# The turned residual on its way through the scratch: written whole, read back in 128-byte runs

## The chip, the core and the metric

The kernel runs on one core of one Trainium2 chip. The metric is the device time of one execution in microseconds (us). Before the change the median of three runs is 1144.76 us (1144.58 to 1144.79). The core has five engines with a queue of instructions each: TensorE (PE, matmuls), VectorE (DVE), ScalarE (ACT), GpSimd (POOL) and SyncE (SP). SyncE does nothing here but issue DMA transfers; ScalarE issues some too, between its own instructions. An engine works through its queue in order, so an instruction that waits holds up all that is queued behind it.

## The reference

A decoder of two layers over 512 tokens and 1024 features, all in f32. Only the end of layer 1 matters here: the residual `h` takes the result of the feed-forward block, then a gated per-layer embedding, then the final norm.

```python
h = h + conv_ffn(rmsnorm(h, norm_ffn[i]), f_w_up[i], f_conv_w[i], f_conv_b[i], f_w_down[i])
h = h + per_layer_embed(h, p[i], norm_ple[i], ple_w_in[i], ple_w_gate[i], ple_b_gate[i])
...
return rmsnorm(h, norm_final)

def per_layer_embed(h, p_i, g_norm, w_in, w_gate, b_gate):
    gate = jax.nn.sigmoid(rmsnorm(h, g_norm) @ w_gate + b_gate)
    return (p_i @ w_in) * gate
```

## The kernel before

**Precision and weights.** Every f32 operand is split into a high and a low part, and a product takes three matmuls (lines 222 to 224, or 233 to 235 with tokens as rows). Weights come in units of up to 128 x 1024. For each unit SyncE loads a raw tile (`wraw`, `load`, lines 155 to 168; six buffers r0 to r5 in rotation), ScalarE makes the high half `wh` with a cast (line 187), and VectorE makes the low half `wl` with a subtraction (line 196). `wh` and `wl` have four buffers each. A raw buffer is free again when its low half is made. `chunk` (line 206) traces the units for the next matmuls and, through `pump`, four units ahead.

**The stage.** In `ffn(1, ...)` the last `dense_add` (lines 366 to 388) runs over four pairs of output tiles. For each of the eight tiles m of 128 features x 512 tokens: matmuls into a PSUM bank `d`, the add into `h[m]` (line 383), the norm's share (`norm.take`: line 280 on ScalarE, 281 on VectorE, 309 on ScalarE, 314 on GpSimd), then a `load` that looks six units ahead (line 387), then `turn_h(m)`. That turns h[m] in blocks of 32 x 32 on VectorE (`nc.vector.transpose`, line 966) into a tile `ht` and hands the tile before it to `write`, which stores it from ScalarE's queue with four DMAs into a scratch tensor `rows` in HBM (lines 956 to 961). `rows` has tokens as rows and features as columns.

**Behind it** the work goes on with tokens as rows. Weights of the gate, W_gate, are 12 units: four through `wh`/`wl`, eight into buffers of their own (`own_ah`, `own_al`). Eight half blocks (4 token blocks x 2 halves of 512 features) go through TensorE; the first two are begun with six of eight features' chunks (lines 984 to 985) and finished later (line 995). `rows` is read back from SyncE's queue by eight DMAs, one a half block (lines 990 to 992), into `hT`. For each half block VectorE makes `z` (line 1010), ScalarE the sigmoid `gs` (line 1016), VectorE multiplies (1017) and adds into `hT` (1019), ScalarE squares (1029). `finish(i)` scales a token block (1058), turns blocks 0 and 1 back (1064) and stores them with 128-byte runs (1067); block 2 goes out as it is (1061). The last block goes out in two pieces (1103).

**What sets the order.** The program is traced in the order of the source; a scheduler then fixes each engine's order when the program is built, by its own estimate of when an instruction is ready, and may move one ahead of others. DMAs share eight completion counters in rotation, over both queues; a DMA waits until the one before it on its counter has landed.

Of the kernel before, what the change touches and what calls it, by code (L numbers as in the profile page):

```python
# [8 lines left out]
F32 = mybir.dt.float32  # L9
# [5 lines left out]
P = 128  # L15
D = 1024
S = 512
KD = D // P
NC = S // P
# [10 lines left out]
SQ = 32  # L30
# [15 lines left out]
RAWS = 6  # L46
# [6 lines left out]
def tile_yoco(ctx: ExitStack, tc: tile.TileContext, t, out: bass.AP, out_b: bass.AP):  # L53
    nc = tc.nc
# [5 lines left out]
    wp = ctx.enter_context(tc.tile_pool(name="wp", bufs=1))  # L60
    mp = ctx.enter_context(tc.tile_pool(name="mp", bufs=1))
    tp = ctx.enter_context(tc.tile_pool(name="tp", bufs=2))
# [3 lines left out]
    def psum(name, tag=None):  # L66
        if tag is None:
            tag = banks["tags"][banks["at"] % len(banks["tags"])]
            banks["at"] += 1
        return mmp.tile([P, S], F32, tag=tag, bufs=4 if tag == "mm" else 1, name=name)  # L70

    def psum2(name):
        return mmp.tile([P, 2, S], F32, tag="sc", name=name)
# [79 lines left out]
    state = {"raw": 0, "unit": 0, "next": 0, "tags": list(range(RAWS)), "turn": 0, "cap": held_back}  # L153

    def load(upto, queue=nc.sync):
        while state["raw"] < min(upto, len(units)):
            j = state["raw"]
            a, m, _ = units[j]
            tags = state["tags"]
            r = wp.tile([P, UNIT], F32, tag=f"r{tags[state['turn'] % len(tags)]}", bufs=1, name=f"wraw{j}")  # L160
            state["turn"] += 1
            if len(a.shape) == 4:
                for c in range(2):
                    queue.dma_start(r[:, :m].rearrange("p (k c n) -> p k c n", c=2, n=256)[:, :, c], a[:, :, c])
            else:
                queue.dma_start(r[:, :m], a)
            raws[j] = r
            state["raw"] += 1
# [37 lines left out]
    def chunk(cols, kk, ahead=WBUFS):  # L206

        pump(state["next"] + ahead)
        parts = []
        while len(parts) < kk:  # L210
            wh, wl, n = take()
            parts += [(wh, wl, j * cols) for j in range(n // cols)]
        assert len(parts) == kk
        return parts

    def mm3(ps, parts, xs, c0, n=P, first=True, last=True):

        for k, ((wh, wl, off), (xh, xl)) in enumerate(zip(parts, xs)):
            a, b = off + c0, off + c0 + n
            st = first and k == 0  # L220
            en = last and k == len(parts) - 1
            nc.tensor.matmul(ps, wh[:, a:b], xh, start=st, stop=False)  # L222
            nc.tensor.matmul(ps, wh[:, a:b], xl, start=False, stop=False)  # L223
            nc.tensor.matmul(ps, wl[:, a:b], xh, start=False, stop=en)  # L224
# [138 lines left out]
    def gain(name, l=0):  # L363
        return lambda k: v(name, l * KD + k)

    def dense_add(xs, kk, norm, fresh=False, then=None):

        for c in range(4):
            parts = chunk(256, kk)
            pss = []  # L370
            if fresh and c == 0:
                pss = [psum(f"d{j}") for j in range(2)]
                for k0, k1 in ((0, kk - 1), (kk - 1, kk)):
                    for j in range(2):
                        mm3(pss[j], parts[k0:k1], xs[k0:k1], j * P, first=k0 == 0, last=k1 == kk)
            for j in range(2):
                m = 2 * c + j
                if pss:
                    ps = pss[j]
                else:  # L380
                    ps = psum(f"d{m}")
                    mm3(ps, parts, xs, j * P)
                nc.vector.tensor_add(h[m], h[m], ps)  # L383
                if norm is not None:
                    norm.take(m)
                if then is not None:
                    load(state["unit"] + RAWS)
                    then(m)

    def ffn(l, norm, nxt, then=None):  # L390
# [35 lines left out]
        for i, (j0, j1) in enumerate(PARTS):  # L426
            act += [up(j) for j in range(j0 + 1, j1)]
            last = j1 == NJ
            if last and l == 0:
                pe = ple_in(l)  # L430
            nact = [] if last else [up(j1)]
            dense_add(act, j1 - j0, nxt if last else None, fresh=last and l > 0, then=then if last else None)
            act = nact
# [67 lines left out]
    for k0, k1 in FIRST:  # L501
        parts = chunk(S, k1 - k0, ahead=1)
        for k in range(k0, k1):
            if k:
                n0.split(k, 0)
            else:
                for c in range(2):
                    s = slice(c * N, (c + 1) * N)
# [57 lines left out]
    for c in range(4):  # L566
# [4 lines left out]
        for j in range(2):  # L571
            m = 2 * c + j
# [9 lines left out]
            s = tp.tile([P, S], F32, tag="c0", name=f"s{m}")  # L582
# [7 lines left out]
            us.append((hi, lo))  # L590
    nf = Norm("nf0", [(xp, "x", gain("norm_ffn", 0))])
    dense_add(us, KD, nf)


    dram = ctx.enter_context(tc.tile_pool(name="dram", bufs=1, space=bass.MemoryType.DRAM))
# [3 lines left out]
    for i, (name, l) in enumerate((("ple_b_gate", 1), ("norm_final", 0))):  # L599
        c0 = VEC[name] + l * KD  # L600
# [12 lines left out]
    at = ctx.enter_context(tc.tile_pool(name="at", bufs=1))  # L613
# [51 lines left out]
    alibi = at.tile([P, GQ, P], F32, tag="alibi", name="alibi")  # L665
# [284 lines left out]
        nf.take(m)  # L950

    npl = Norm("np1", [(xp, "x", gain("norm_ple", 1))])
    rows = dram.tile([S, D], F32, name="rows")
    queue = []

    def write(m, t):

        for q in range(P // SQ):
            c0 = m * P + q * SQ
            nc.scalar.dma_start(rows[:, c0 : c0 + SQ].rearrange("(b i) j -> i b j", i=SQ),  # L960
                              t[q * SQ : (q + 1) * SQ, :].rearrange("p (b j) -> p b j", j=SQ))

    def turn_h(m):

        t = tp.tile([P, S], F32, tag=f"c{m % 2}", name=f"ht{m}")
        nc.vector.transpose(t, h[m])
        if queue:
            write(*queue.pop())
        queue.append((m, t))

    ffn(1, nf, npl, turn_h)
    write(*queue.pop())

    xs = npl.xs[0][0]
# [1 line left out]
    for i, r in enumerate((brow, grow)):  # L976
        nc.sync.dma_start(r.rearrange("p (m q) -> p m q", m=KD), lines[:, i, :].partition_broadcast(P))
    turned_h = at.tile([P, NC - 1, S], F32, tag="vd", name="hT")
    hT = [turned_h[:, q, :] for q in range(NC - 1)] + [at.tile([P, S], F32, tag="alibi", name="hT3")]
    hT = [hT[:2], hT[2:]]  # L980

    parts = chunk(S, KD)
    pss = [psum(f"gate{i}", "mm") for i in range(2)]
    for i in range(2):
        mm3t(pss[i], xs[:6], parts[:6], 0, S, i, last=False)
    parts2 = chunk(S, KD)
    for i in range(2):
        r = wp.tile([P, D], F32, tag=f"r{4 + i}", bufs=1, name=f"hT{2 + i}")
        hT.append([r[:, :S], r[:, S:]])
    for i in range(NC):  # L990
        for c in range(2):
            nc.sync.dma_start(hT[i][c], rows[i * P : (i + 1) * P, c * S : (c + 1) * S])
    ms = psum2("ms")[:, 0, :NC]
    for i in range(2):
        mm3t(pss[i], xs[6:], parts[6:], 0, S, i, first=False)
# [35 lines left out]
    def mean(i, n, out_):  # L1031

        nc.vector.tensor_reduce(out_, ssq[:, i, :n], axis=mybir.AxisListType.X, op=ALU.add)
        nc.vector.tensor_scalar(out_, out_, 1.0 / D, EPS, op0=ALU.mult, op1=ALU.add)

    def root(i):

        r = rfin[:, i : i + 1]
        nc.gpsimd.tensor_tensor(r, total[:, i : i + 1], minus_half[:, :1], op=ALU.pow)
        return r  # L1040

    flat = out.rearrange("k p s -> (k p) s")
# [10 lines left out]
    def finish(i):  # L1053

        mean(i, 2, total[:, i : i + 1])
        r = root(i)
        for c in range(2):
            nc.vector.scalar_tensor_tensor(hT[i][c], hT[i][c], r, grow[:, c * S : (c + 1) * S],
                                           op0=ALU.mult, op1=ALU.mult)
            if i == 2:  # L1060
                nc.sync.dma_start(out_b[0, :, c * S : (c + 1) * S], hT[i][c])
                continue
            t = tp.tile([P, S], F32, tag=f"c{c}", name=f"y{i}_{c}")
            nc.vector.transpose(t, hT[i][c])
            for q in range(P // SQ):
                s0 = i * P + q * SQ
                nc.sync.dma_start(flat[c * S : (c + 1) * S, s0 : s0 + SQ].rearrange("(f c) a -> c f a", c=SQ),
                                  t[q * SQ : (q + 1) * SQ, :].rearrange("p (f a) -> p f a", a=SQ))

    for i in range(2):  # L1070
# [1 line left out]
    for i in range(2):  # L1072
        half(i, 1)
        finish(i)
    for c in range(2):
        half(2, c)
    finish(2)
    half(end, 0)
    nc.gpsimd.tensor_mul(yt[:, :S], hT[end][0], grow[:, :S])

    others = const.tile([P, 1], F32, name="others")
    with in_order(*engines[1:]):
# [12 lines left out]
        r = root(end)  # L1095
        nc.vector.tensor_mul(yt[:, S + N :], hm, grow[:, S + N :])
        for q, (c0, c1) in enumerate(((0, 384), (384, D))):
            y = yt[:, c0:c1]
# [71 lines left out]
```

## Time and profile before

| | before |
|---|---|
| median of three runs | 1144.76 us |
| the profiled execution, its own time | 1144.59 us |
| its span from the first to the last instruction | 1142.9 us |
| mean granted TensorE clock | 0.994 |
| HBM read, written | 110.33 MB, 4.20 MB |

The span is that of the profiled execution; what lies around it, 1.7 us, is in its time and not in the trace. Rows of a timeline read: start and duration in us, engine, line, operation, output<-inputs, shape, count, and in brackets the idle time before it with what ended it. An engine name with a q (ACTq, SPq) stands for its sequencer, here for the issue of DMAs. Rows of DMA issues read: output<-input, queue, kind, count, size of each, median us from issue to landing. Rows of windows read: the stretch, its length, then busy time and count (x) for PE, PEld, DVE, ACT and POOL, the granted clock, the DMA engines' share and GB/s; with a filter on one engine only that one stands there. The granted clock is a share of full speed.

```profile
PEclk9999999999999999999999999999999999999998
DMA  9322322322323333332054324433223233323443
```

These are two of the rows in 40 equal slices: the clock in tenths of full speed, and the share of the 16 DMA engines. The stage above lies in the last four slices.

### The profile page before, as it was taken

Reading aid. Unit: us, or ns where it says so; the run is one execution under the profiler, and the core shown is the slowest. Engines: PE = TensorE matmul, PEld = TensorE weight load, DVE = VectorE, ACT = ScalarE, POOL = GpSimd, SP = SyncE. Lnnn points to the kernel's source line nnn. Section 1 sums busy time; section 2 is a strip of 40 time slices with the busy share of each in tenths; the row PEclk is TensorE's granted clock in tenths of the full one; section 3 lists DMA queues with packets and bytes.
Section 4 is the critical chain, followed back from the end, with each engine's and each line's share of the span. In section 5 each row is a group of like instructions: output and inputs, shape, how many; then the busy total and the mean of one; then the engine's idle time right before and its main releaser. Section 6 shows DMA issues by size and latency. Waiting matters only on the chain.

```text
span 1142.9 us, 13466 instructions
## 1 busy us (share of the span) xinstructions
PE 1123.6 (98%) x5116; PEld 932.2 (82%) x5116; DVE 736.2 (64%) x974; ACT 505.4 (44%) x801; POOL 134.6 (12%) x160
## 2 busy tenths in 40 slices
PE   9999999999999999999999999999999999999895
PEld 7888888888888888888898887888888888888675
DVE  7356467762677367557858887677636773677556
ACT  6533344441343244445756776544413432344342
POOL 2100210000000000022235564100000000000101
PEclk9999999999999999999999999999999999999998
DMA  9322322322323333332054324433223233323443
GB/s 319 110 94 81 104 89 96 111 92 92 109 69 100 111 109 88 99 111 94 18 147 129 93 93 166 136 104 111 86 98 103 73 102 111 102 70 113 90 124 74
DMA packets 70097, 120.66 MB, mean 106 GB/s; under 512 B 30344, under 2 KB 41104, under 8 KB 70032
## 3 DMA queue, kind: packets, MB, share of 16 engines
q1 hardware_dynamic: 52704, 117.24, 32.5%
q10 hardware_dynamic: 17328, 2.56, 1.2%
q8 instruction: 40, 0.66, 0.2%
q14 instruction: 25, 0.20, 0.1%
HBM read 110.33 MB, written 4.20 MB: 100 GB/s over the span
## 4 chain that ended last, share of the span: by engine, by line
PE 93%; DVE 2%; DMA 1%; issue 1%; ACT 1%; ACTq 0%; SPq 0%; POOL 0%; POOLq 0%
PE up L222 14%; PE up L224 14%; PE up L223 14%; PE d L224 8%; PE d L223 8%; PE d L222 8%; PE o L222 1%; PE q L222 1%; PE o L223 1%; PE o L224 1%; PE sc L738 1%; PE q L224 1%; PE gate L222 1%; PE q L223 1%; PE u L222 1%
## 5 line engine op out<-in xcount | busy, mean ns | idle before, releaser
L196 DVE TENSOR_TENSOR wl<-wraw,wh 128x1024 fp32r<-128x1024 f32 (+2 forms) x197 | 239.5, 1218 | 117.9 <-ACT wh L187 117.3
L187 ACT CAST wh<-wraw 128x1024 fp32r<-128x1024 f32 (+1 forms) x196 | 201.7, 1032 | 245.9 <-PE d L223 132.8
L224 PE MATMUL d<-ah,wl 128*128 128x512 f32 x352 | 137.8, 391 | 2.2 <-DVE wl L196 2.2
L223 PE MATMUL d<-al,wh 128*128 128x512 f32 x352 | 137.6, 391 | 0.0
L222 PE MATMUL d<-ah,wh 128*128 128x512 f32 x352 | 137.5, 391 | 0.0
L222 PE MATMUL up<-nf00h,wh 128*128 128x512 f32 x352 | 137.1, 390 | 0.0
L222 PE MATMUL up<-nf10h,wh 128*128 128x512 f32 x352 | 137.0, 389 | 0.0
L224 PE MATMUL up<-nf00h,wl 128*128 128x512 f32 x352 | 137.0, 389 | 0.0
L223 PE MATMUL up<-nf00l,wh 128*128 128x512 f32 x352 | 136.9, 389 | 0.0
L224 PE MATMUL up<-nf10h,wl 128*128 128x512 f32 x352 | 136.9, 389 | 0.0
L223 PE MATMUL up<-nf10l,wh 128*128 128x512 f32 x352 | 136.9, 389 | 0.0
L412 ACT ACTIVATE c<-hs,vec 128x512 f32<-128x512 f32 x88 | 71.8, 816 | 88.9 <-DVE hs L408 87.9
L413 DVE SCALAR_TENSOR_TENSOR c<-hs,vec,c 128x511 f32<-128x511 f32 x88 | 65.9, 748 | 37.4 <-ACT c L412 37.2
L383 DVE TENSOR_TENSOR h<-h,d 128x512 f32<-128x512 f32 x56 | 38.4, 686 | 79.7 <-PE d L224 79.7
L224 PEld LDWEIGHTS d<-ah,wl 128*128 128x128 f32 x352 | 66.4, 189 | 16.4 <-DVE wl L196 2.6
L222 PEld LDWEIGHTS d<-ah,wh 128*128 128x128 f32 x352 | 66.5, 189 | 13.9
L223 PEld LDWEIGHTS d<-al,wh 128*128 128x128 f32 x352 | 66.4, 189 | 13.9
L284 ACT CAST ah<-a 128x512 fp32r<-128x512 f32 x44 | 27.4, 622 | 113.5 <-DVE a L418 113.5
L224 PEld LDWEIGHTS up<-nf10h,wl 128*128 128x128 f32 x352 | 66.1, 188 | 13.8
L222 PEld LDWEIGHTS up<-nf00h,wh 128*128 128x128 f32 x352 | 66.1, 188 | 13.7
L223 PEld LDWEIGHTS up<-nf00l,wh 128*128 128x128 f32 x352 | 66.1, 188 | 13.7
L223 PEld LDWEIGHTS up<-nf10l,wh 128*128 128x128 f32 x352 | 66.1, 188 | 13.7
(289 smaller groups left out, 1976.1 us busy)
## 6 DMA issues: line engine op xcount, KB each, us to landing
wraw<-in_w_up SPq DMA_DIRECT2D x88, 512.0 KB, 3.5
wraw<-in_w_down SPq DMA_DIRECT2D x32, 512.0 KB, 3.5
wraw<-in_w_down SPq DMA_DIRECT2D x16, 384.0 KB, 3.3
wraw<-in_w_u SPq DMA_DIRECT2D x8, 512.0 KB, 7.7
wraw<-in_w_out SPq DMA_DIRECT2D x8, 512.0 KB, 3.5
wraw<-in_w_gate SPq DMA_DIRECT2D x8, 512.0 KB, 3.8
wraw<-in_w_q SPq DMA_DIRECT2D x8, 512.0 KB, 3.5
wraw<-in_w_o SPq DMA_DIRECT2D x8, 512.0 KB, 3.2
```

The lines of the kernel that those rows point to most:

```text
L187: nc.scalar.copy(wh[:, :n], src)
L196: nc.vector.tensor_sub(wl[:, :n], src, wh[:, :n].bitcast(F32))
L222: nc.tensor.matmul(ps, wh[:, a:b], xh, start=st, stop=False)
L223: nc.tensor.matmul(ps, wh[:, a:b], xl, start=False, stop=False)
L224: nc.tensor.matmul(ps, wl[:, a:b], xh, start=False, stop=en)
L284: nc.scalar.copy(hi, src)
L383: nc.vector.tensor_add(h[m], h[m], ps)
L412: nc.scalar.activation(c, hs, AF.Identity, bias=v("conv_b", l * 2 * NJ + col), scale=cw[2])
L413: nc.vector.scalar_tensor_tensor(c[:, 1:], hs[:, : S - 1], cw[1], c[:, 1:], op0=ALU.mult, op1=ALU.add)
L738: nc.tensor.matmul(o[:, e, 2 * P - nk :], q, x[g // 2][:, g % 2, t0 : t0 + nk], start=st, stop=not st)
```

## The change

`rows` becomes eight tiles of 128 x 512 as VectorE's transpose leaves them, and each is stored with a single DMA in rows of 2 KB. What the four DMAs of a tile sorted out on the way in is sorted out on the way back: each token block is read by four DMAs of 32 partitions, each made of 32 x 32 runs of 128 bytes. These 16 reads are each pinned on SyncE's queue behind what was traced there before, so behind all loads of weights. The buffers of the read blocks change: block 0 in the tile `hT`, blocks 1 to 3 in r3, r4 and r5. The look-ahead of loads in `dense_add` is taken out. Blocks 0 and 1 of the output are turned into one whole tile each (r0, r1) and stored with four DMAs in place of eight.

```diff
                 if then is not None:
-                    load(state["unit"] + RAWS)
                     then(m)
...
-    rows = dram.tile([S, D], F32, name="rows")
+    rows = dram.tile([KD, P, S], F32, name="rows")
...
     def write(m, t):
 
-        for q in range(P // SQ):
-            c0 = m * P + q * SQ
-            nc.scalar.dma_start(rows[:, c0 : c0 + SQ].rearrange("(b i) j -> i b j", i=SQ),
-                              t[q * SQ : (q + 1) * SQ, :].rearrange("p (b j) -> p b j", j=SQ))
+        nc.scalar.dma_start(rows[m], t)
...
-    hT = [turned_h[:, q, :] for q in range(NC - 1)] + [at.tile([P, S], F32, tag="alibi", name="hT3")]
-    hT = [hT[:2], hT[2:]]
+    full = [turned_h[:, :2, :].rearrange("p a s -> p (a s)")]
...
-    for i in range(2):
-        r = wp.tile([P, D], F32, tag=f"r{4 + i}", bufs=1, name=f"hT{2 + i}")
-        hT.append([r[:, :S], r[:, S:]])
+    full += [wp.tile([P, D], F32, tag=f"r{2 + i}", bufs=1, name=f"hT{i}") for i in range(1, NC)]
+    hT = [[x[:, :S], x[:, S:]] for x in full]
+    back = rows.rearrange("k (p a) s -> a (k p) s", a=SQ)
     for i in range(NC):
-        for c in range(2):
-            nc.sync.dma_start(hT[i][c], rows[i * P : (i + 1) * P, c * S : (c + 1) * S])
+        for q in range(P // SQ):
+            s0 = i * P + q * SQ
+            tc.keep_in_program_order(nc.sync.dma_start(
+                full[i][q * SQ : (q + 1) * SQ, :].rearrange("a (f j) -> a f j", j=SQ), back[:, :, s0 : s0 + SQ]))
...
+        t = wp.tile([P, D], F32, tag=f"r{i}", bufs=1, name=f"y{i}") if i < 2 else None
         for c in range(2):
...
-            t = tp.tile([P, S], F32, tag=f"c{c}", name=f"y{i}_{c}")
-            nc.vector.transpose(t, hT[i][c])
+            nc.vector.transpose(t[:, c * S : (c + 1) * S], hT[i][c])
+        if i < 2:
             for q in range(P // SQ):
                 s0 = i * P + q * SQ
-                nc.sync.dma_start(flat[c * S : (c + 1) * S, s0 : s0 + SQ].rearrange("(f c) a -> c f a", c=SQ),
+                nc.sync.dma_start(flat[:, s0 : s0 + SQ].rearrange("(f c) a -> c f a", c=SQ),
                                   t[q * SQ : (q + 1) * SQ, :].rearrange("p (f a) -> p f a", a=SQ))
```

## The prediction

> **What bounds the kernel now.** I read first the share of each engine, then the chain that ended last, then TensorE's waits over the whole span.
>
> ```profile
> span 1142.9 us, 13466 instructions
> PE 1123.6 (98%) x5116; PEld 932.2 (82%) x5116; DVE 736.2 (64%) x974; ACT 505.4 (44%) x801; POOL 134.6 (12%) x160
> PE 93%; DVE 2%; DMA 1%; issue 1%; ACT 1%; ACTq 0%; SPq 0%; POOL 0%; POOLq 0%
> ...
> PE gate L235 <- DVE wl L196: 3.0, 2, 2.2
> PE d L224 <- DVE wl L196: 2.2, 1, 2.2
> ```
>
> TensorE sets the time. The last two rows head its list (total wait, number of waits, longest, in us); what follows them there belongs to the start of the kernel. It stands still three times only, and each time for the same thing: wl, the low half of a weight unit, which VectorE makes on line 196. All three lie in the stage that the change edits. The timeline of TensorE around them, then its busy time and granted clock in the stretches between (the digits after the busy time are the count of matmuls, then the clock):
>
> ```profile
> 1067.83 0.39 PE L223 MATMUL d<-al,wh 128*128 128x512 f32 x1
> 1070.40 0.50 PE L224 MATMUL d<-ah,wl 128*128 128x512 f32 x1 [2.18 <-DVE wl L196]
> ...
> 1074.85 0.39 PE L224 MATMUL d<-ah,wl 128*128 128x512 f32 x1
> ...
> 1081.20 0.39 PE L233 MATMUL gate<-wh,np10h 128*128 128x512 f32 x1
> 1081.43 0.39 PE L234 MATMUL gate<-wh,np10l 128*128 128x512 f32 x1
> 1083.99 0.50 PE L235 MATMUL gate<-wl,np10h 128*128 128x512 f32 x1 [2.18 <-DVE wl L196]
> ...
> 1088.44 0.40 PE L235 MATMUL gate<-wl,np10h 128*128 128x512 f32 x1
> ...
> 1095.78 0.50 PE L235 MATMUL gate<-wl,np10h 128*128 128x512 f32 x1 [0.81 <-DVE wl L196]
> ...
> 1070.40:1074.80 4.40, 4.40 (x12) 0.61 0.54 140
> 1083.90:1088.40 4.50, 4.41 (x12) 0.62 0.59 153
> ```
>
> From 1074.85 to 1081.20 lie 28 undisturbed steps: 0.227 us each. Stall A: a step of 2.57 (2.34 lost), then 12 steps in 4.45 where 2.72 would do (1.73 lost), because the granted clock fell to 0.61. A costs 4.07 us. Stall B: 2.33 + 1.73 = 4.06. Stall C: 0.8, with no loss of clock that I count. Together **8.9 us**, all that TensorE could get back here.
>
> Why wl is late shows on VectorE and ScalarE:
>
> ```profile
> 1061.01 1.79 ACT L187 CAST wh<-wraw 128x1024 fp32r<-128x1024 f32 x2 [0.75 <-issue]
> 1068.53 0.71 DVE L966 STREAM_TRANSPOSE ht<-h 128x512 f32<-128x512 f32 x1
> 1069.17 1.18 DVE L196 TENSOR_TENSOR wl<-wraw,wh 128x1024 fp32r<-128x1024 f32 x1
> 1072.80 3.44 ACTq L960 DMA_DIRECT2D rows<-ht  x4
> 1076.28 1.05 ACT L187 CAST wh<-wraw 128x1024 fp32r<-128x1024 f32 x1 [6.51 <-DMA rows<-ht]
> 1082.12 0.71 DVE L966 STREAM_TRANSPOSE ht<-h 128x512 f32<-128x512 f32 x1
> 1082.76 1.18 DVE L196 TENSOR_TENSOR wl<-wraw,wh 128x1024 fp32r<-128x1024 f32 x1
> 1086.31 5.60 ACTq L960 DMA_DIRECT2D rows<-ht  x8
> 1091.95 1.05 ACT L187 CAST wh<-wraw 128x1024 fp32r<-128x1024 f32 x1 [8.59 <-DMA rows<-ht]
> ```
>
> ScalarE's cast must precede wl. The casts of the last two weight columns stand behind the issues of rows on ScalarE's queue: 6.51 us idle before one pair, 8.59 before the next. A and B have a second cause. VectorE works through a fixed order, and there wl stands behind the next tile's add and transpose (1068.53, then 1069.17; 1082.12, then 1082.76), though for A its cast was done by 1061.01 + 1.79 = 1062.80. The same loop of layer 0, without transposes and writes, has another order: cast, at once wl, then the add:
>
> ```profile
> 495.13 1.06 ACT L187 CAST wh<-wraw 128x1024 fp32r<-128x1024 f32 x1 [0.52 <-PE d L223]
> 496.22 1.22 DVE L196 TENSOR_TENSOR wl<-wraw,wh 128x1024 fp32r<-128x1024 f32 x1 [1.35 <-ACT wh L187]
> 497.39 0.69 DVE L383 TENSOR_TENSOR h<-h,d 128x512 f32<-128x512 f32 x1
> ```
>
> None of TensorE's three waits falls in layer 0. I take it that the 32 writes crowd ScalarE in the order that was fixed when the program was built, and that this pushed wl back there.
>
> **The change, part by part.**
>
> ```profile
> rows<-ht ACTq DMA_DIRECT2D x32, 64.0 KB, 1.9
> wraw<-in_w_gate SPq DMA_DIRECT2D x8, 512.0 KB, 3.8
> row_m<-lines SPq DMA_DIRECT2D x2, 512.0 KB, 6.2
> out<-hT SPq DMA_DIRECT2D x2, 256.0 KB, 2.1
> q10 hardware_dynamic: 17328, 2.56, 1.2%
> 1095.75 3.84 SPq L164 DMA_DIRECT2D wraw<-in_w_gate  x8
> 1114.44 11.34 SPq L1067 DMA_DIRECT2D out<-y  x16
> 1130.41 1.01 SPq L1061 DMA_DIRECT2D out<-hT  x2
> ```
>
> *Writes.* 32 issues of 512 runs of 128 bytes become 8 issues of 128 rows of 2 KB. The nearest row is the store of half a token block, 256 KB in 2 KB rows: two issues within 1.01 us, landing after 2.1. The last eight issues took 5.60 us; two in their place take 1.0, so the casts for C start some 4.6 us earlier. The rest of the 8.59 us is a wait on a completion counter: of eight in rotation, 32 writes use up four rounds and so meet the counters of loads that were issued just before and still wait for their buffer; 8 writes use up one. So each pair of tiles frees ScalarE of six issues at 0.7 us, and of such a wait. That is more than C's 0.8, and with it goes, as I read layer 0, the order behind A and B. Bounds: 0 (wl stays where it is, since the transposes on VectorE are kept) to 8.9. I take A and B whole, because the layer 0 order is the nearest that the trace has, and half of C, because its two units can only be cast when the last down matmuls release their buffers: 4.07 + 4.06 + 0.4 = **8.5 us**.
>
> By the Trainium skill, page "TensorE: Matmul & The Clock Gate" (What's actually happening), the clock halves after about one idle window of 3.4 us, so gaps of 2.2 us should cost nothing beyond themselves; the saving would be 2.34 + 2.33 + 0.4 = 5.1 us. The rows above disagree: the clock stood at 0.61 and 0.62 behind both gaps.
>
> *The look-ahead that is removed* (line 387): it only traced loads earlier. SyncE issues loads as raw buffers come free, and a load waits for its buffer in both versions. Cost 0, covered by the release; if SyncE ran late, a load would cost its landing, 3.8 us, once.
>
> *Reads.* 8 reads of 2 KB rows become 16 of 1024 runs of 128 bytes, 16384 runs, four reads a token block. No row shows such a read. From below: the packets of queue 10 took 1.2% of 16 engines' span, 219 us over 17328 packets, 12.7 ns each; 64 a read and engine make 0.81 us, **3.2 us a block**. From above: the two broadcast reads of 1024 runs of 512 bytes that land together 6.2 us after issue: 3.1 us a read, **12.4 a block**. I take the eight writes of 512 runs in 5.60 us, **5.6 a block**: same run, same queue hardware, only the direction differs.
>
> *The pin.* The reads stand behind the last weight load. Today that group ends at 1095.75 + 3.84 = 1099.6; with A and B gone it moves with TensorE by at least 8.1, to 1091.5 or earlier. Queued behind the reads on SyncE are only the stores of the output. VectorE waits for the blocks at line 1019; its rows today, and the share of VectorE in that stretch:
>
> ```profile
> 1106.44 1.29 DVE L1019 TENSOR_TENSOR hT<-hT,gs 128x512 f32<-128x512 f32 x2
> 1117.07 0.69 DVE L1019 TENSOR_TENSOR hT<-hT,gs 128x512 f32<-128x512 f32 x1
> 1124.30 0.69 DVE L1019 TENSOR_TENSOR hT<-hT,gs 128x512 f32<-128x512 f32 x1
> 1131.96 0.68 DVE L1019 TENSOR_TENSOR hT<-hT,gs 128x512 f32<-128x512 f32 x1
> 1100.00:1129.00 29.00, 29.00 (x144) 24.64 (x143) 20.77 (x36) 11.22 (x23) 1.10 (x2) 1.00 0.40 93
> ```
>
> Less 8.1 they are due at 1098.3 and 1099.0 (blocks 0 and 1, first row, two adds), 1116.2 (block 2) and 1123.9 (block 3). Block i lands at 1091.5 + 5.6(i+1) + 1.9: 1099.0, 1104.6, 1110.2, 1115.8. So block 1 holds VectorE up by 5.6 us, behind it the next z and its PSUM bank. VectorE has 29.0 - 20.8 = 8.2 us idle in this stretch and TensorE six banks to run ahead in, so I cost it at 0; without that cover 5.6. Blocks 2 and 3 are early.
>
> *The output stores* are 8 of 1024 runs in place of 16 of 512, the same bytes. Today they end at 1114.44 + 11.34 = 1125.8, 4.6 us before SyncE's next store at 1130.41, and that room hides a like number of runs: 0. If they ran later than that, the store at 1130.41 would wait for them. *The tail* behind TensorE's last matmul is the same work; a shared-port clash of VectorE and GpSimd in it may come or go, for which I leave 1 us on both sides.
>
> **Sum.** The profiled execution took 1144.59: 1142.9 span and 1.7 around it (the median of the runs is 0.2 above it). 1144.6 - 8.5 = **1136.1 us**.
>
> **Rivals.**
>
> *Late reads (slower).* If a 128-byte read goes at the pace of the broadcast rows, block 3 lands at 1091.5 + 49.6 + 1.9 = 1143.0, 19.1 us behind its need; 1136.1 + 19.1 = **1155 us**. For: nothing shows short reads from HBM to be as quick as short writes. Against: those rows carried four times the bytes a run, in company of weight loads. It decides from 1123.9 + 8.5 = 1091.5 + 4x + 1.9, x = 9.8 us a block; below that the change still gains. The Trainium skill, page "DMA: Bandwidth & Descriptors" (Specifications), asks for 512 bytes and more a transfer and speaks of a read-modify-write below that; the rows here have 128-byte writes alone, at 12.7 ns, and no run shows the reads.
>
> *One stall stays.* wl keeps its place behind the transpose for A or for B: 1144.6 - 4.1 - 0.4 = **1140 us**. For: both transposes remain, each 0.71 us. Against: layer 0 shows room for wl before the add.
>
> *The change doesn't do what it says.* The order hangs on the transposes, not on the writes. Reads start at 1099.6, block 3 lands at 1099.6 + 22.4 + 1.9 = 1123.9, before 1131.96: **1144.6 us**.
>
> *The clock rule holds* and the gaps alone are saved, 5.1 us: 1144.6 - 5.1 = **1139.5 us**. Against it stand the two clock rows.
>
> **Chances.** Forecast 0.52, late reads 0.20, one stall stays 0.15, no effect 0.10, clock rule 0.03. A measurement of this kernel tells about 0.2% (2.3 us) from no change. Faster: 0.52 + 0.15 + 0.03 = 0.70. Same: 0.09 of the no-effect case. Slower: 0.20 and the rest, 0.21. The range reaches down to all of 8.9 us and 1 us in the tail (1134.7, put at 1134) and up to 1151, between the break-even of late reads and their full price; the likeliest case alone spans 1134 to 1138.
>
> **What would show it.** Right: TensorE's list of waits loses both rows of 2.2 us, the clock reads 1.00 through the stage, eight issues of rows on ScalarE take 0.3 to 0.5 us each with no cast idle behind them, and wl stands ahead of the add on VectorE. The reads start near 1091, a block takes 5.6 us, and line 1019 waits for hT only once. Wrong: a wait of z or gs on hT<-rows late in the stage (late reads), or wl still behind a transpose with TensorE's 2.2 us in place (order unchanged).

## The result and the profile after

The changed kernel takes 1140.82 us (median of seven runs, 1140.65 to 1141.10); the kernel before took 1143.92 us beside it (1142.16 to 1144.79). The ratio is 0.9975, with a 95% interval of 0.9963 to 0.9986: a gain of about 3 us where 8.5 were forecast. The profiled execution took 1141.05 us, its span 1139.3 us.

First TensorE after the change. Its group of gate matmuls with the weights' own low halves (count, shortest/median/longest in ns, first and last start), and the window that held the stalls (columns as before):

```profile
L235 PE MATMUL gate<-own_al,np10h x40: 279/389/389, 1089.6 to 1122.0; 128*128 128x512 f32 x24, 128*128 128x256 f32 x16
```

```profile
1050.00:1090.00 40.00, 40.00 (x182) 33.27 (x181) 29.84 (x41) 21.17 (x32) 9.73 (x7) 1.00 0.53 150
```

And VectorE's timeline around one pair of splits, with the issues of the writes:

```profile
1066.89 1.23 DVE L196 TENSOR_TENSOR wl<-wraw,wh 128x1024 fp32r<-128x1024 f32 x1 [1.03 <-ACT wh L187]
1068.07 0.69 DVE L383 TENSOR_TENSOR h<-h,d 128x512 f32<-128x512 f32 x1
1068.93 1.23 DVE L196 TENSOR_TENSOR wl<-wraw,wh 128x1024 fp32r<-128x1024 f32 x1 [0.17 <-ACT wh L187]
```

```profile
rows<-ht ACTq DMA_DIRECT2D x8, 256.0 KB, 2.4
```

TensorE is busy without a gap from 1050 to 1090 at the full clock, wl stands ahead of the add, and the last matmul starts at 1122.0. The same group in the kernel before:

```profile
L235 PE MATMUL gate<-own_al,np10h x40: 279/389/390, 1101.4 to 1131.0; 128*128 128x512 f32 x24, 128*128 128x256 f32 x16
```

So TensorE ends 9.0 us earlier, all that the forecast said it could get back. But the span shrank by 3.6 us only (1142.9 to 1139.3): 5.4 us are lost again behind TensorE. VectorE's timeline after the change shows where:

```profile
1100.27 0.75 DVE L1007 SCALAR_TENSOR_TENSOR z<-gate,np1rt,row_m 128x512 f32<-128x512 f32 x1 [4.09 <-PE gate L235]
...
1105.71 0.75 DVE L1007 SCALAR_TENSOR_TENSOR z<-gate,np1rt,row_m 128x512 f32<-128x512 f32 x1 [1.97 <-PE gate L235]
1111.15 0.75 DVE L1007 SCALAR_TENSOR_TENSOR z<-gate,np1rt,row_m 128x512 f32<-128x512 f32 x1 [4.69 <-PE gate L235]
1111.82 1.29 DVE L1016 TENSOR_TENSOR hT<-hT,gs 128x512 f32<-128x512 f32 x2
...
1126.04 1.42 DVE L1056 SCALAR_TENSOR_TENSOR hT<-hT,rfin,row_m 128x512 f32<-128x512 f32 x2 [0.65 <-POOL rfin L1036]
...
1133.64 0.55 DVE L1098 TENSOR_SCALAR yt<-yt,rfin 128x640 f32<-128x640 f32 x1 [0.44 <-POOL rfin L1036]
```

The waits of VectorE and of SyncE in the last stage (total, number, longest):

```profile
DVE z L1007 <- PE gate L235: 13.6, 4, 4.7
...
SPq L1101 <- DMA out<-yt: 8.3, 1, 8.3
```

The two adds into hT at 1111.82 belong to block 1. They stand behind the z of later half blocks, and each of these z waits for TensorE. VectorE idles 13.6 us in four such waits, then has much of its work left when TensorE stops. Its last instruction ends at 1133.64 + 0.55 = 1134.19, against 1138.98 before:

```profile
1138.43 0.55 DVE L1100 TENSOR_SCALAR yt<-yt,rfin 128x640 f32<-128x640 f32 x1 [0.44 <-POOL rfin L1039]
```

That is 4.8 us earlier, 4.2 less than TensorE's 9.0. And the last store is not issued when VectorE is done. ScalarE's and SyncE's timelines at the end:

```profile
1134.29 0.34 ACTq L1101 DMA_DIRECT2D out<-yt  x1
...
1136.24 0.33 SPq L1101 DMA_DIRECT2D out<-yt  x1
```

SyncE issues it 2.05 us after VectorE's end (before: at 1139.01, 0.03 after), because it first waits for ScalarE's store of the other part to land. From that issue to the end of the span it is 3.1 us in place of 3.9. 4.2 + 2.0 - 0.8 = 5.4 us: the whole loss.

The reads had no part in it by their time. SyncE's timeline after the change, and the issues of the reads:

```profile
1041.14 39.37 SPq L164 DMA_DIRECT2D wraw<-in_w_gate  x22
1083.87 13.27 SPq L988 DMA_DIRECT2D hT<-rows  x16
```

```profile
hT<-rows SPq DMA_DIRECT2D x16, 128.0 KB, 4.3
```

```profile
SPq L988 <- DMA rows<-ht: 3.2, 1, 3.2
```

All weights are issued by 1080.5. The reads then wait 3.2 us more for a write of `rows` to land (last row), since each of them takes values from all eight tiles. They begin at 1083.87, and four of them (one block) take 13.27 / 4 = 3.3 us. With 4.3 us to landing the last is in at about 1101, ahead of the adds at 1111.82, and no add of VectorE waits for a read.

### The profile page after: what moved, and what is told of

It is laid out like the page before. It is cut to its first block, busy times and chain, and to the rows that moved or that the text cites. A ratio compares the mean times of both kernels' runs of the same rounds, so it can differ in the third digit from the quotient of the medians.

```text
span 1139.3 us, 13456 instructions
## 1 busy us (share of the span) xinstructions
PE 1119.9 (98%) x5116; PEld 930.4 (82%) x5116; DVE 734.4 (64%) x974; ACT 505.2 (44%) x801; POOL 134.8 (12%) x160
## 4 chain that ended last, share of the span: by engine, by line
PE 96%; DVE 1%; DMA 1%; issue 0%; ACT 0%; SPq 0%; POOL 0%; POOLq 0%; DVEq 0%; ACTq 0%
PE up L224 14%; PE up L222 14%; PE up L223 14%; PE d L224 8%; PE d L223 8%; PE d L222 8%; PE o L222 1%; PE o L223 1%; PE q L222 1%; PE sc L737 1%; PE o L224 1%; PE q L224 1%; PE gate L222 1%; PE q L223 1%; PE u L222 1%; PE gate L223 1%
## 5 line engine op out<-in xcount | busy, mean ns | idle before, releaser
L222 PEld LDWEIGHTS up<-nf10h,wh 128*128 128x128 f32 x352 | 66.1, 188 | 13.7
L224 PEld LDWEIGHTS up<-nf00h,wl 128*128 128x128 f32 x352 | 66.1, 188 | 13.6
```

## The experiments

Two questions were open: what put VectorE's last stage in that order, and what had really removed the stalls. The table gives each run's median, its ratio to the kernel before on the same chip with the 95% interval, then from its profile the span, the start of TensorE's last matmul and the end of VectorE's last instruction (all in us). Runs 4, 10 and 11 read the values back in another arrangement, so they serve the measurement alone and don't compute the output.

| run | time | ratio | span | last matmul | VectorE's end |
|---|---|---|---|---|---|
| before | 1143.92 | 1 | 1142.9 | 1131.0 | 1138.98 |
| after | 1140.82 | 0.9975 (0.9963 to 0.9986) | 1139.3 | 1122.0 | 1134.19 |
| 1 text's order in the last stage | 1133.68 | 0.9912 (0.9899 to 0.9926) | 1131.5 | 1121.5 | 1126.38 |
| 2 both last stores on SyncE | 1139.49 | 0.9963 (0.9951 to 0.9976) | 1137.8 | 1121.9 | 1134.05 |
| 3 both of these | 1132.20 | 0.9900 (0.9886 to 0.9913) | 1130.6 | 1121.9 | 1126.82 |
| 4 long reads | 1133.20 | 0.9908 (0.9895 to 0.9922) | 1131.4 | 1121.8 | 1127.59 |
| 5 four issues a tile | 1144.02 | 1.0002 (0.9993 to 1.0011) | 1142.5 | 1122.0 | 1137.29 |
| 6 after, with look-ahead | 1140.88 | 0.9973 (0.9964 to 0.9983) | 1139.2 | 1121.9 | 1134.03 |
| 7 before, no look-ahead | 1144.29 | 1.0003 (0.9994 to 1.0013) | 1142.5 | 1130.6 | 1138.57 |
| 8 before, text's order | 1146.96 | 1.0026 (1.0016 to 1.0036) | 1145.3 | 1131.5 | 1141.48 |
| 9 before, reads pinned | 1145.27 | 1.0015 (1.0006 to 1.0024) | 1141.7 | 1129.0 | 1137.76 |
| 10 before, 32 writes of 2 KB runs | 1134.50 | 0.9923 (0.9908 to 0.9938) | 1133.6 | 1122.4 | 1129.69 |
| 11 before, 8 whole writes | 1132.86 | 0.9908 (0.9891 to 0.9924) | 1131.2 | 1121.6 | 1127.44 |
| 12 before, two pairs of splits first | 1136.87 | 0.9938 (0.9925 to 0.9952) | 1135.2 | 1123.1 | 1131.26 |

### Where the gain went: runs 1 to 4

Theory: VectorE's order in the last stage was fixed when the program was built, by a scheduler that held the short-run reads to be slow, and the last store lost 2 us more on a counter. Rival: the reads themselves, landing late or crowding the stage. Run 1 takes the order of VectorE and ScalarE from the source:

```diff
-    for i in range(2):
-        half(i, 0)
+    with in_order(*engines[1:3]):
+        for i in range(2):
+            half(i, 0)
...
-    half(end, 0)
+        half(end, 0)
```

> Only the order of VectorE and ScalarE in the last stage is taken from the program text; every transfer stays. If that order holds the gain back: VectorE's 13.6 us of waits on the gate's matmuls in front of the adds into hT go, VectorE's last instruction ends some 8 us behind TensorE's last matmul, as in the kernel before, in place of 11.9, and the span falls by 3.5 to 4.5 us, to about 1135; the last store still waits 2.0 us for ScalarE's. If the short-run reads land late or crowd the last stage: VectorE then waits on the reads at the first adds into hT and the span stays at 1139 or grows.

The head of VectorE's list of waits from 1085 us on in that run:

```profile
DVE gs L1014 <- ACT gs L1013: 4.7, 7, 0.7
DVE np1m L355 <- PE ms L995: 2.6, 1, 2.6
```

Its timeline, with the first finish and the last row, and SyncE's last store:

```profile
1099.04 0.75 DVE L1056 SCALAR_TENSOR_TENSOR hT<-hT,rfin,row_m 128x512 f32<-128x512 f32 x1 [0.66 <-POOL rfin L1036]
...
1125.83 0.55 DVE L1099 TENSOR_SCALAR yt<-yt,rfin 128x640 f32<-128x640 f32 x1 [0.43 <-POOL rfin L1036]
...
1128.42 0.33 SPq L1102 DMA_DIRECT2D out<-yt  x1
```

The 13.6 us of waits for the gate are gone, block 0 is finished at 1099, and the span falls by 7.8 us, twice what was expected: VectorE ends 4.9 us behind the start of the last matmul, where even the kernel before needed 8.0. The same reads, as short and as late, hold nothing up here, so the rival falls. The last store still waits 2.0 us (VectorE's end at 1126.38, issue at 1128.42). Run 2:

```diff
-            (nc.sync if q else nc.scalar).dma_start(out_b[1, :, c0:c1], y)
+            nc.sync.dma_start(out_b[1, :, c0:c1], y)
```

> Both final stores on SyncE's queue. If the last store waits for the counter that it shares with ScalarE's store: the 2.0 us between the end of VectorE's last instruction and its issue go, less up to 0.4 us for the second issue, so 1.6 to 2.0 us less than the changed kernel, about 1137.5 in the span. If it waits for something else, such as the data or SyncE's earlier stores: no change, 1139.3.

It gained 1.5 us in the span and 1.3 in the time, just under what was expected; the two stores now leave back to back as soon as the data stand (two issues from 1134.14 in SyncE's row). Run 3 has both edits:

> The text's order in the last stage and both final stores on SyncE's queue. If the two losses are separate: the two gains add up, 5 to 6.5 us less than the changed kernel, a span of 1133 to 1134, and so 9 to 10 us less than the kernel before. If one hides the other: no more than the larger of the two alone.

1132.20 us, 1.5 below run 1: the two losses are separate and nearly add up (8.7 us in the span; 7.8 and 1.5 alone). The span of 1130.6 lies below the 1133 to 1134 expected, because run 1's share was larger. This is the best version here that computes the output, 11.0 us below the kernel before of its chip (1143.22). Run 4 asks what made the scheduler choose the order. It leaves it free and changes only the reads:

```diff
-    back = rows.rearrange("k (p a) s -> a (k p) s", a=SQ)
+    back = rows.rearrange("k (r a) s -> (k r) (a s)", a=2)
...
-                full[i][q * SQ : (q + 1) * SQ, :].rearrange("a (f j) -> a f j", j=SQ), back[:, :, s0 : s0 + SQ]))
+                full[i][q * SQ : (q + 1) * SQ, :], back[s0 : s0 + SQ, :]))
```

> The 16 reads fetch contiguous rows of 4 KB, so that the values are not sorted back and hT holds other data; writes, queue and look-ahead are those of the changed kernel. If the scheduler's price of the short runs makes the order of the last stage: VectorE's adds follow each half block again, its 13.6 us of waits in front of them go and the span falls by 3 to 5 us, to about 1135, while the stalls of TensorE stay away, since the writes are whole. If the short runs cost only through their transfer: the reads land sooner but VectorE's order and the 1139 stay. If the turned writes alone are not what removed the stalls, some of the 8 us of stalls returns.

VectorE's only wait for the gate in that run, one half block from its z to its add, and SyncE's first reads with the loads behind them:

```profile
DVE z L1007 <- PE gate L235: 1.6, 1, 1.6
```

```profile
1109.10 0.71 DVE L1007 SCALAR_TENSOR_TENSOR z<-gate,np1rt,row_m 128x512 f32<-128x512 f32 x1
1110.51 0.69 DVE L1014 TENSOR_TENSOR gs<-gs,pet 128x512 f32<-128x512 f32 x1 [0.70 <-ACT gs L1013]
1111.23 0.69 DVE L1016 TENSOR_TENSOR hT<-hT,gs 128x512 f32<-128x512 f32 x1
```

```profile
1065.22 0.89 SPq L988 DMA_DIRECT2D hT<-rows  x2
1067.89 0.83 SPq L164 DMA_DIRECT2D wraw<-in_w_gate  x2
```

With these reads each add follows its own half block again, and the span falls by 7.9 us, more than the 3 to 5 expected. So the order that was built around the reads, not their time on the chip, took the gain away. What in the reads made that order is not shown, because this edit changes two things at once. The runs grow from 128 bytes to 4 KB, and each read now needs half of one tile in place of a piece of all eight. The second can be seen at work: four reads go out between 1065 and 1071, ahead of the last eight loads (so the pin alone doesn't put them behind all loads). That the scheduler priced the short runs high is thus only one of two readings; the other is that it held reads of all eight tiles to be ready late.

### What removed the stalls: runs 5 to 12

The forecast held that 32 issues on ScalarE delay its casts. Run 5 keeps the changed kernel's layout and reads, but writes each tile with four DMAs:

```diff
-        nc.scalar.dma_start(rows[m], t)
+        for q in range(P // SQ):
+            nc.scalar.dma_start(rows[m, q * SQ : (q + 1) * SQ, :], t[q * SQ : (q + 1) * SQ, :])
```

> Each residual tile goes out in four transfers of 32 partitions with 2 KB runs, 32 issues on ScalarE's queue as in the kernel before, to the same place and with the same reads as in the changed kernel. If the number of issues on ScalarE delayed the halves of the weights: VectorE's splits slide behind the adds again, TensorE waits for wl once to three times, 4 to 9 us, its last matmul starts between 1126 and 1131 in place of 1122.0, and the span grows to between 1141 and 1147. If the 128-byte runs of the writes did it: no waits, the last matmul at 1122 and a span of 1139.3.

There are 32 issues again and no stall: TensorE's last matmul starts at 1122.0. So it isn't the number. The span of 1142.5 lies where the theory of the number put it, but by another way: VectorE ends 15.3 us behind the last matmul, 3.1 more than after the change. The reads begin at 1090.45 in place of 1083.87, and the order in the last stage is worse still. Its first add into hT, then the first add after the change:

```profile
1104.04 0.68 DVE L1017 TENSOR_TENSOR hT<-hT,gs 128x512 f32<-128x512 f32 x1
```

```profile
1095.50 0.68 DVE L1016 TENSOR_TENSOR hT<-hT,gs 128x512 f32<-128x512 f32 x1
```

The reads have the same runs in both kernels; only the writes before them differ. So the order of the last stage doesn't hang on the runs of the reads alone.

Runs 6 and 7 put the look-ahead back into the changed kernel, and take it out of the kernel before:

```diff
                 if then is not None:
+                    load(state["unit"] + RAWS)
                     then(m)
```

> The changed kernel with the extra look-ahead at weights put back. If the writes alone took the stalls away: the same span within 0.5, 1139.3, and no wait of TensorE for wl. If the look-ahead made the stalls, by loads that came too early: some of the 8 us return.

> The kernel before with only the extra look-ahead taken out. If the writes make the stalls: TensorE waits 5.2 us for wl as before, a span of 1142 to 1143 and the time of the kernel before within 1 us. If the look-ahead made them: no wait for wl and 5 to 8 us less.

Both are what they were without the edit (1140.88 against 1140.82; 1.0003 of the kernel before, with its 5.2 us of waits): the look-ahead does nothing. Run 8 is run 1's edit in the kernel before:

> The kernel before with VectorE and ScalarE in the text's order in the last stage. If the scheduler's order cost time in the kernel before too: VectorE's last instruction ends 4 to 6 us behind TensorE's last matmul in place of 7.7, and the span falls by 2 to 4 us to about 1140; TensorE's waits for wl stay. If that order was as good as the text's: the same span within 1 us, so that the 4.6 us of the changed kernel in the text's order have another source.

This expectation failed in both its forms: the span grew by 2.4 us, and VectorE ended 10.0 us behind the last matmul. The text's order isn't better as such. A likely reason, which no run tests, is that VectorE enters the last stage with arrears. In the kernel before it is still busy with splits at 1103:

```profile
1096.78 3.22 DVE L196 TENSOR_TENSOR own_al<-wraw,own_ah 128x512 fp32r<-128x512 f32 x5
...
1103.28 0.69 DVE L196 TENSOR_TENSOR own_al<-wraw,own_ah 128x512 fp32r<-128x512 f32 x1
```

In the changed kernel these are done 19 us earlier, at 1085.2:

```profile
1083.91 1.30 DVE L196 TENSOR_TENSOR own_al<-wraw,own_ah 128x512 fp32r<-128x512 f32 x2 [0.57 <-ACT own_ah L187]
```

Run 9 does the pin alone, run 10 the long runs alone (the number of writes and the reads of the kernel before), run 11 the whole writes with unpinned long reads:

```diff
-            nc.sync.dma_start(hT[i][c], rows[i * P : (i + 1) * P, c * S : (c + 1) * S])
+            tc.keep_in_program_order(nc.sync.dma_start(hT[i][c], rows[i * P : (i + 1) * P, c * S : (c + 1) * S]))
```

> The kernel before with its eight reads of 2 KB runs kept behind all loads of weights on SyncE's queue; the writes stay 32 of 128-byte runs, and VectorE's order is that of the kernel before. If VectorE's order makes TensorE's waits: wl is late as before, 5.2 us of waits, a span of 1142 to 1144. If the reads that stand among the loads on SyncE's queue hold the loads, and through them the casts: the waits shrink by half or more and the span falls by 3 to 8 us.

```diff
-    rows = dram.tile([S, D], F32, name="rows")
+    rows = dram.tile([2, NC, NC, SQ, S], F32, name="rows")
...
+            nc.scalar.dma_start(rows[m // NC, q, m % NC], t[q * SQ : (q + 1) * SQ, :])
...
+            nc.sync.dma_start(hT[i][c], rows[c, i].rearrange("k p s -> (k p) s"))
```

> The kernel before with the same 32 writes by partitions of 32, but each to a stretch of its own in the scratch, so in 2 KB runs, and the same eight reads of 2 KB runs; the values come back in another arrangement, so hT holds other data. If the length of the runs of the writes made the waits: no wait of TensorE for wl, its last matmul near 1122. If the number of writes did: the waits of the kernel before, and 1142 to 1143. If the waits go and the last stage keeps the order of the kernel before: a span of 1133 to 1137.

```diff
-    rows = dram.tile([S, D], F32, name="rows")
+    rows = dram.tile([KD, P, S], F32, name="rows")
...
+        nc.scalar.dma_start(rows[m], t)
...
+            nc.sync.dma_start(hT[i][c], rows[c * NC + i])
```

> The kernel before with eight whole writes and eight contiguous reads of 256 KB, not pinned and with the look-ahead in place; hT holds other data. If the whole writes alone take the waits away and the reads' short runs alone spoil the last stage: TensorE's last matmul near 1122 and a span of 1130 to 1134, as with long reads in the changed kernel. If the pin or the tiles that the blocks moved to were needed for it: waits of TensorE for wl, or reads among the loads that delay them, and a span of 1135 or more.

TensorE's waits for wl in run 9:

```profile
PE gate L235 <- DVE wl L196: 3.0, 2, 2.2
PE d L224 <- DVE wl L196: 2.2, 1, 2.2
```

The group of gate matmuls in runs 9, 10 and 11, in this order:

```profile
L235 PE MATMUL gate<-own_al,np10h x40: 279/389/389, 1099.4 to 1129.0; 128*128 128x512 f32 x24, 128*128 128x256 f32 x16
```

```profile
L235 PE MATMUL gate<-own_al,np10h x40: 279/389/389, 1093.2 to 1122.4; 128*128 128x512 f32 x24, 128*128 128x256 f32 x16
```

```profile
L235 PE MATMUL gate<-own_al,np10h x40: 279/389/389, 1089.3 to 1121.6; 128*128 128x512 f32 x24, 128*128 128x256 f32 x16
```

The pin leaves all waits in place, and the time over ten runs is 0.15% longer, so it gains nothing. That TensorE ends 2 us earlier in its one profile has another source, which shows when the clock is read behind the gaps A and B as in the forecast:

```profile
1069.99 0.50 PE L224 MATMUL d<-ah,wl 128*128 128x512 f32 x1 [2.18 <-DVE wl L196]
1069.90:1074.30 4.40, 4.31 (x19) 1.00 0.46 130
1081.90:1086.40 4.50, 4.41 (x12) 0.62 0.57 148
```

Gap A is as long as before, but the clock behind it stays at 1.00, and 19 matmuls run where 12 ran; behind gap B it falls to 0.62 as before. So a gap of 2.18 us is not followed by the slow clock each time. In the profiles of before and runs 7, 8 and 9, seven of eight such gaps were, by a clock of 0.50 or 0.51 over some 3 us; what decides is not shown.

Longer runs at the same 32 issues (run 10) remove the waits. Eight whole writes with long reads (run 11) bring 10.4 us, with neither pin nor moved buffers nor the missing look-ahead. That left one fork: do short writes hurt on the chip, or again through the order that was built for them? Run 12 keeps the 32 writes of 128-byte runs and sets only the places of two pairs of splits on VectorE (`h_at` and `wl_at` hold the traced adds and splits; ScalarE's and SyncE's orders come out unchanged):

```diff
     ffn(1, nf, npl, turn_h)
+    last = len(units)
+    for m, first in ((5, last - 14), (7, last - 12)):
+        for u in (first, first + 1):
+            tc.add_manual_dep(h_at[m], wl_at[u].name, mybir.DependencyInfo(
+                mybir.DependencyClass.NoSync, mybir.DependencyReason.DATA), reason="in_order")
```

VectorE's order as built, read from the timelines: adds of tiles 2 to 7 with their transposes (T) and the splits into wl between:

```
before, 9    add2 T add3 T add4 T add5 T wl wl add6 T add7 T wl wl
5, 10, 12    add2 T add3 T add4 T wl wl add5 T add6 T wl wl add7 T
after, 11    add2 T wl add3 wl T add4 T wl add5 wl T add6 T wl add7 wl T
```

This part of the order goes with the shape of the writes: runs 5 and 10 share it though their reads differ, and so do after, 4 and 11.

> The kernel before, its 32 writes of 128-byte runs and its reads as they are, and the order of ScalarE and SyncE too; only two pairs of splits into wl are placed ahead of the next add into h on VectorE (ahead of the adds of tiles 5 and 7), as in the run with 32 writes of 2 KB runs. If the short runs hurt only through the order that the scheduler chose for them: TensorE's waits of 2.2 us for wl go, its last matmul starts between 1122 and 1124, and the span is 1133 to 1136 with the last stage in the order of the kernel before. If the short runs hurt on the chip, by ScalarE's issues and its waits for completion counters in front of the casts: the casts stay late, at least one wait of 2.2 us stays, and the span is 1138 to 1143.

TensorE's only wait for wl in run 12, one of the moved pairs on VectorE, and the group of gate matmuls:

```profile
PE gate L237 <- DVE wl L197: 0.8, 1, 0.8
```

```profile
1065.25 3.18 DVE L197 TENSOR_TENSOR wl<-wraw,wh 128x1024 fp32r<-128x1024 f32 x2
1068.35 0.74 DVE L283 SCALAR_TENSOR_TENSOR np10l<-h,vec,np10h 128x512 fp32r<-128x512 f32 x1
1069.02 0.67 DVE L385 TENSOR_TENSOR h<-h,d 128x512 f32<-128x512 f32 x1
```

```profile
L237 PE MATMUL gate<-own_al,np10h x40: 279/389/389, 1093.4 to 1123.1; 128*128 128x512 f32 x24, 128*128 128x256 f32 x16
```

Both waits of 2.2 us are gone and only C's 0.8 is left, with every short write still there; the time falls by 7.6 us (1144.43 to 1136.87), more than twice what the change itself brought. So the short writes did not cause A and B on the chip; the order that was built for them did, with two pairs of splits one add too late. Run 10 shows that the length of their runs is what changed that order; that the scheduler prices a DMA by its runs is the likely way, and not shown. C is another matter: it stays with the short writes and is gone with the long ones of run 10.

## Why the prediction was partly wrong

**The stalls (A, B and half of C, 8.5 us): size right, with some luck.** TensorE's last matmul starts 9.0 us earlier, against 8.9 for all three. (C was counted by its idle time; by its step, like A and B, it is 0.98: 1094.57 to 1095.78, less 0.23.) Run 12, which removes A and B alone, moves the last matmul by 7.9, against 8.13 forecast for the two. The gaps alone would give 2.34 + 2.33 = 4.7, so the slow clock is part of the price. But all these differences are taken from the one profile of the kernel before, which had the slow clock behind both gaps. In run 9's it followed one only, which makes the stalls about 1.7 us cheaper. That may also be why the times of the kernel before spread over 2.6 us and those of the changed kernel over 0.45; only the profiled executions have a trace, so this is not shown.

**Their cause: half right.** That the writes push wl back through the order fixed at the build held, and so did the reading that wl stands behind the next tile's add and transpose. The count of issues and counters fell for A and B: run 10 has the 32 issues without the waits, run 12 the short runs too. ScalarE's waits of 6.51 and 8.59 us were real, but not what bound there: run 12 still has one of 4.3 us, and it costs C's 0.8.

**Look-ahead 0, pin 0: right** (runs 6 and 7; run 9 for the pin, tested with the reads of the kernel before).

**Reads: 5.6 us a block taken, 3.3 measured**, close to the lower bound of 3.2. They started at 1083.87 rather than 1091.5: the splits, and with them the weight loads, moved by more than TensorE did, and what held the reads in the end was not the loads but a write, for 3.2 us. Late reads fell as a rival: no add waited for one.

**The last stage: the step that failed.** Two sentences carried it: block 1's wait costs nothing since VectorE has "8.2 us idle in this stretch", and "the tail behind TensorE's last matmul is the same work". Both took VectorE's order for given. The work is the same, but the scheduler arranged it otherwise around the new reads, so VectorE's idle time became 13.6 us in front of work that stood ready, and its end lost 4.2 us. Another 2.0 went to the last store, which waited for ScalarE's, and 0.8 came back. Run 1 shows it: with VectorE and ScalarE in the text's order, and the same transfers, the span falls by 7.8 us. That the order is fixed at the build stood in the forecast as the reason for the stalls; it was not asked of the stage into which the new reads go.

**The rivals.** "One stall stays" named 1140 us, close to the time, but by luck: no stall stayed. "Doesn't do what it says" fell, since order and stalls did change. The clock rule named 1139.5 and falls too: it allows TensorE 5.1 us, and it got 9.0. The Trainium skill's page "TensorE: Matmul & The Clock Gate" (What's actually happening) puts the idle window at about 3.4 us; the gaps of 2.2 us here were followed by 0.61 and 0.62 of the clock, and removing them gave more than the gaps. So the measurement decides against the rule at this length, with the limit that run 9 shows: one gap as long left the clock at 1.00.

## What to carry to other kernels

When a DMA's shape changes, or what it needs before it can start, ask what the scheduler will make of it on every engine that uses the data: read the built order before and after, above all where an instruction stands behind one that waits for another engine. A transfer that is fast on the chip can still cost microseconds through the place that was given to its users, and one order constraint may be worth more than the new transfer. At the end of a kernel, see that the last store waits only for its data.

## What the runs showed of the hardware

Sixteen reads of 1024 runs of 128 bytes went out at 0.83 us each (13.27 / 16), 128 KB at a time, and landed 4.3 us after issue; with runs of 4 KB twelve of them took 5.44 us, 0.45 each, and 3.2 us to land:

```profile
1084.22 5.44 SPq L988 DMA_DIRECT2D hT<-rows  x12
```

```profile
hT<-rows SPq DMA_DIRECT2D x12, 128.0 KB, 3.2
```

So runs of 128 bytes from HBM cost less than twice what long ones do in issue. A gap of 2.18 us in TensorE's work was followed by some 3 us at a granted clock of 0.50 or 0.51 in seven of eight cases, at a price of 1.73 us each in the two that were counted. The two kernels that differ only in the queue of one store at the end (after and run 2) show what a wait for another queue's store costs there: 1.5 us.
